# Gate and up of both FFNs by seven block products, with tokens in two phases

## The chip, the cores and the metric

The kernel runs on one core of a Trainium2 chip. The metric is device microseconds for one execution: the median of three runs before the change is 2480.66 us (2476.45 to 2481.32). Engines are TensorE (PE, with its weight loads as PEld), VectorE (DVE), ScalarE (ACT), GpSimd (POOL) and SyncE (SP), which issues most of the DMAs.

## The reference, cut to what matters

The reference is one layer of a decoder for 1024 prompt tokens and 64 sample tokens, that is 1088 rows x of 1024 channels, all float32:

```
x += 1/2 * SwiGLU_1(rms(x))
h = rms(x); [q | k | v | u | g_a | g_b] = h @ w_in
x += (sigmoid(g_a) * (A @ w_attn_branch) + sigmoid(g_b) * (B @ w_pool_branch)) @ w_out
x += 1/2 * SwiGLU_2(rms(x))

def _swiglu(x, w_up, w_down):
    gate, up = jnp.split(x @ w_up, 2, axis=-1)
    return (jax.nn.silu(gate) * up) @ w_down
```

A is a dilated attention and B a pooling over u; the change does not touch them. An FFN has 2816 hidden channels, so w_up is 1024 x 5632 and w_down 2816 x 1024. Key, value and pooling caches are copied to the outputs, in DMAs from DRAM to DRAM.

## The kernel before, in words

Channels lie on partitions and tokens on the free dimension. `xt` holds the residual as 8 blocks of 128 channels x 1088 tokens. Tokens are cut into three chunks, `CH`: 360, 360 and 368.

*Precision.* Each float32 operand is split into two float32r tiles: `hi` by an ACT copy, `lo` by a subtraction on DVE (`split`, lines 214 to 216; for the normed activations one in three is on POOL, line 341). `mm3` (lines 264 to 271) makes of each block pair three matmuls: hi x hi, hi x lo, lo x hi, summed in PSUM. So a block of 128 output channels with 1024 input channels costs 8 x 3 matmuls per chunk.

*Norm.* `norm` squares x on ACT, adds the squares on DVE and POOL, sums over partitions with small matmuls, takes the inverse root on DVE (`rsqrt`, 11 tiny operations) and writes a diagonal matrix `dg`; `normed` spreads it over partitions with one matmul and multiplies x, gain and that result on DVE, then splits it into `h_hi` and `h_lo`.

*FFN* (`ffn`, lines 344 to 432). Eleven steps `j`, each for 256 hidden channels: `wunit` loads gate's weights and splits them; six `gate` products (two halves x three chunks) go to PSUM tag `psa` and through Silu on ACT; `down` of the step before then adds its part to x (PSUM tag `psb`, one `scalar_tensor_tensor` on DVE for each of 8 blocks x 3 chunks); then `wunit` for up and six `up` products, which DVE multiplies with Silu's result and `split` stores as `hh`, `hl`. The last `down` goes chunk by chunk and calls `hook`, which starts the next norm or the outputs. PSUM tags `psa` and `psb` have four banks each.

*Memory.* `fp`, the FFN's pool, is opened on the right side after `bp` and `ip` are closed, the pools of the start (position biases: `tb`, `oh`, `fr`; input rows: `xn`, `sq`, `dg`), and so lies in their memory. `biases()` (line 444) makes four rows `fr` and POOL writes them to `f_scr`; 40 DMAs from there to `b_scr` are also on POOL's queue (lines 508 to 518).

*Order.* `Interleaver` puts steps of background jobs (norms, attention, fetches) between products, by costs in us that the code gives. A scheduler then orders the instructions of each engine: an instruction whose inputs are ready can be put ahead of earlier ones that wait; program order is its priority. Each engine and each DMA queue then runs in that order.

Output (`emit_outs`, line 1247): TensorE transposes x, DVE or ACT copies it, POOL and SP write it out.

Of the kernel before, what the change touches and what calls it, by code (L numbers as in the profile page):

```python
# [11 lines left out]
F32 = mybir.dt.float32  # L12
# [8 lines left out]
P = 128  # L21
# [8 lines left out]
CH = ((0, 360), (360, 360), (720, 368))  # L30
AW = 768
# [86 lines left out]
def body(ctx, tc, x_prompt, x_sample, c128, c512, c2048, state_pool, rel_bias_table,  # L118
# [182 lines left out]
    def norm(xt, c, gi):  # L301
        c0, n = CH[c]
# [24 lines left out]
        yield 5
        normed(xt, c, gi, dg)

    def normed(xt, c, gi, dg):  # L330

        c0, n = CH[c]
        r = psb()[:, :n]
        PE.matmul(r, ones, dg, start=True, stop=True)
# [9 lines left out]
    def ffn(xt, w_up, w_down, ncopy, hook):  # L344
        fctx = ExitStack()
        fp = fctx.enter_context(tc.tile_pool(name="fp", bufs=1, side="right"))

        def down(j, hh, hl, last):
            raws, pcs = [], {}
            for f in range(2):  # L350
                r = fp.tile([P, D], F32, tag="dr", name="dr", bufs=2)
                load(r, w_down[(2 * j + f) * P:(2 * j + f + 1) * P, :])
                raws.append(r)
            some_copies(ncopy)
            for dq in range(4):
                for f in range(2):
                    ph = fp.tile([P, 256], F32R, tag="dh", name="dh", bufs=8)
                    pl = fp.tile([P, 256], F32R, tag="dl", name="dl", bufs=8)
                    split(ph, pl, raws[f][:, dq * 256:(dq + 1) * 256])
                    pcs[dq, f] = (ph, pl)  # L360

            def one(d, c):
                c0, n = CH[c]
                o = psb()[:, :n]
                sl = slice((d % 2) * P, (d % 2 + 1) * P)
                mm3(o, [(pcs[d // 2, f][0][:, sl], pcs[d // 2, f][1][:, sl],
                         hh[:, f, c0:c0 + n], hl[:, f, c0:c0 + n]) for f in range(2)])
                xd = xt[:, d, c0:c0 + n]
                V.scalar_tensor_tensor(out=xd, in0=o, scalar=0.5, in1=xd, op0=ALU.mult, op1=ALU.add)  # L369
                il.advance(0.92)  # L370

            if last:
                for c in range(3):
                    for d in range(KD):
                        one(d, c)
                        hook(c, d)
            else:
                for d in range(KD):
                    for c in range(3):
                        one(d, c)  # L380

        def gate(w, f, c):
            o = proj(w, f, c, h_hi, h_lo)
            t = tmp()[:, :CH[c][1]]
            S.activation(t, o, AF.Silu)  # L385
            go()
            return t

        def up(w, f, c, t, hh, hl):
            c0, n = CH[c]  # L390
            o = proj(w, f, c, h_hi, h_lo)
            V.tensor_tensor(out=t, in0=t, in1=o, op=ALU.mult)  # L392
            split(hh[:, f, c0:c0 + n], hl[:, f, c0:c0 + n], t)
            go()

        def wblock(c0, pool):

            w = [pool.tile([P, KD, P], F32R, tag=x, name=x) for x in ("wh", "wl")]
            raw = wp.tile([P, KD, P], F32, tag="wr", name="wr", bufs=3)
            load(raw, w_up[:, c0:c0 + P].rearrange("(k p) n -> p k n", p=P))  # L400
            for k0 in range(0, KD, 4):
                split(w[0][:, k0:k0 + 4, :], w[1][:, k0:k0 + 4, :], raw[:, k0:k0 + 4, :])
            return w

        prev = None
        for j in range(11):
            sil = {}
            if prev is None:
                wg, wu = [wblock(0, wp)], [wblock(DFF, wp)]
            else:  # L410
                wg = wunit(w_up[:, j * 256:(j + 1) * 256])
                for f in range(2):
                    for c in range(3):
                        sil[f, c] = gate(wg, f, c)
                down(*prev, False)
                wu = wunit(w_up[:, DFF + j * 256:DFF + (j + 1) * 256])
            hh = fp.tile([P, 2, T], F32R, tag="hh", name="hh")
            hl = fp.tile([P, 2, T], F32R, tag="hl", name="hl")
            if prev is None:
                for c in range(3):  # L420
                    for f in range(2):
                        if len(wg) == f:
                            wg.append(wblock(P, wp))
                            wu.append(wblock(DFF + P, fp))
                        up(wu, f, c, gate(wg, f, c), hh, hl)
            else:
                for f in range(2):
                    for c in range(3):
                        up(wu, f, c, sil[f, c], hh, hl)
            prev = (j, hh, hl)  # L430
        down(*prev, True)
        fctx.close()

# [33 lines left out]
    for c, (c0, n) in enumerate(CH):  # L467
        tiles = range(3 * c, 3 * c + 3)
        for t in tiles:
            rows = P if t < 8 else NS  # L470
            sq = ip.tile([P, D], F32, tag="sq", name="sq", bufs=1)
            S.activation(sq[:rows], xns[t][:rows], AF.Square, accum_out=st[:rows, 0, t:t + 1])
# [13 lines left out]
        ts = slice(3 * c, 3 * c + 3)  # L486
# [3 lines left out]
        dg = ip.tile([P, 368], F32, tag="dg", name="dg", bufs=2)[:, :n]  # L490
        t0 = c0
        while t0 < c0 + n:
            t, a = t0 // P, t0 % P
            m = min(P - a, c0 + n - t0)
            V.tensor_scalar(out=dg[:, t0 - c0:t0 - c0 + m], in0=ident[:, a:a + m],
                            scalar1=st[:, 1, t:t + 1], scalar2=None, op0=ALU.mult)
            t0 += m
        normed(xt, c, 0, dg)
        if c == 2:
            biases()  # L500
# [26 lines left out]
    def hook1(c, d):  # L527
        if d < KD - 1:
            return
        spill(c)  # L530
        norms[c] = il.spawn(norm(xt, c, 1))
# [780 lines left out]
```

## Time and profile before

| | |
|---|---|
| median of 3 runs | 2480.66 us (2476.45 to 2481.32) |
| the profiled execution | 2476.46 us, span 2474.7 us, mean granted TensorE clock 0.98 |
| busy: PE, DVE, ACT, POOL | 2417.1, 1100.6, 616.6, 180.5 us |
| DMA | 259.11 MB, mean 105 GB/s |
| FFN1 | from the start to about 840 us |
| FFN2 | from about 1665 us to the end |

A row of a group of instructions names line, engine, operation, out<-in with the tile names (buffer numbers left out), shapes, count, then busy us and mean ns of one, then idle time before them. A row of a timeline gives start (us from the span's start), length in us, engine, line and count; in brackets the idle time before it and what ended it. Merged rows say x and a number; the length is then that of all. The record of an operation runs on for some 80 to 90 ns into the next on DVE, so operations back to back are closer than their length.

### The profile page before, as it was taken

To read this page: it belongs to the slowest core of one execution; us is meant where nothing else is said; L and a number is where in the kernel's file an instruction comes from. 1 tells how busy PE (TensorE), PEld (TensorE's weight loads), DVE (VectorE), ACT (ScalarE), POOL (GpSimd) and SP (SyncE) were. 2 spreads that over 40 slices of the span, in tenths; PEclk is the share of its full clock that TensorE was granted. 3 is DMA by queue.
4 is the path that set the end of the run, shared out by engine and by line. 5 is a ranking of instruction groups with operands and counts; after the bars stand their busy time and mean duration, and the time that the engine had idled before them with its cause. 6 is when DMAs were issued, how large, how long until landed. Compare 5 with 4: busy or idle time off the path is not lost.

```text
span 2474.7 us, 35899 instructions
## 1 busy us (share of the span) xinstructions
PE 2417.1 (98%) x14820; PEld 2364.7 (96%) x14820; DVE 1100.6 (44%) x2317; ACT 616.6 (25%) x1436; POOL 180.5 (7%) x304
## 2 busy tenths in 40 slices
PE   5999999999999899999899999999999999999999
PEld 4999999999999899999889799999999999999998
DVE  6244333333433743466677226545333333443334
ACT  5211111111111333434343132233111221111111
POOL 4200000000000211110011110011000000000001
PEclk7999999999999999999999999999999999999999
DMA  4411212222120223376654944710211222222132
GB/s 134 142 43 60 85 33 71 85 85 86 68 86 18 100 62 111 128 219 196 194 185 153 317 156 150 250 52 18 85 69 35 85 86 85 69 85 84 33 113 73
DMA packets 159571, 259.11 MB, mean 105 GB/s; under 512 B 14160, under 2 KB 128528, under 8 KB 158624
## 3 DMA queue, kind: packets, MB, share of 16 engines
q1 hardware_dynamic: 145392, 224.26, 27.8%
q0 software_dynamic: 14016, 32.56, 3.8%
q8 instruction: 116, 1.90, 0.3%
q14 instruction: 47, 0.39, 0.1%
HBM read 227.89 MB, written 76.32 MB: 123 GB/s over the span
## 4 chain that ended last, share of the span: by engine, by line
PE 85%; issue 6%; DVE 3%; DMA 3%; POOL 1%; ACT 1%; SPq 0%; POOLq 0%; DVEq 0%; ACTq 0%
PE psa L269 21%; PE psa L270 20%; PE psa L271 20%; PE psb L270 7%; PE psb L271 7%; PE psb L269 7%; DMA qb<-q_scr 1%; DMA u_scr<-us 1%; DMA wr<-in_ffn_w_up_dram 1%; DMA rt<-u_scr 1%; PE psb L745 1%; DVE qb L904 0%; PE psb L1065 0%; PE psb L879 0%; DVE sc L906 0%
## 5 line engine op out<-in xcount | busy, mean ns | idle before, releaser
L269 PE MATMUL psa<-h_hi,wh 128*128 128x360 f32 (+1 forms) x3216 | 1070.5, 333 | 22.9 <-DVE hl L216 13.1
L270 PE MATMUL psa<-h_lo,wh 128*128 128x360 f32 (+1 forms) x3216 | 1066.1, 332 | 5.3 <-DVE h_lo L341 5.1
L271 PE MATMUL psa<-h_hi,wl 128*128 128x360 f32 (+1 forms) x3216 | 1063.7, 331 | 0.0
L269 PEld LDWEIGHTS psa<-h_hi,wh 128*128 128x128 f32 x3216 | 612.0, 190 | 33.6 <-ACT wh L215 16.4
L270 PEld LDWEIGHTS psa<-h_lo,wh 128*128 128x128 f32 x3216 | 611.8, 190 | 10.9 <-DVE h_lo L341 5.9
L271 PEld LDWEIGHTS psa<-h_hi,wl 128*128 128x128 f32 x3216 | 611.4, 190 | 3.6 <-issue 2.8
L216 DVE TENSOR_TENSOR wl<-wr,wh 128x512 fp32r<-128x512 f32 (+1 forms) x284 | 185.9, 683 | 523.7 <-ACT wh L215 523.4
L369 DVE SCALAR_TENSOR_TENSOR xt<-psb,xt 128x360 f32<-128x360 f32 (+1 forms) x528 | 281.9, 534 | 262.5 <-PE psb L271 262.1
L269 PE MATMUL psb<-hh,dh 128*128 128x360 f32 (+1 forms) x1056 | 348.1, 330 | 0.0
L270 PE MATMUL psb<-hl,dh 128*128 128x360 f32 (+1 forms) x1056 | 348.1, 330 | 0.0
L271 PE MATMUL psb<-hh,dl 128*128 128x360 f32 (+1 forms) x1056 | 347.3, 329 | 0.0
L215 ACT ACTIVATE wh<-wr 128x512 fp32r<-128x512 f32 (+1 forms) x284 | 162.7, 618 | 381.4 <-PE psa L270 367.7
L269 PEld LDWEIGHTS psb<-hh,dh 128*128 128x128 f32 x1056 | 199.4, 189 | 0.3 <-DVE xt L369 0.2
L270 PEld LDWEIGHTS psb<-hl,dh 128*128 128x128 f32 x1056 | 198.9, 188 | 0.2
L271 PEld LDWEIGHTS psb<-hh,dl 128*128 128x128 f32 x1056 | 199.1, 189 | 0.0
L215 ACT ACTIVATE dh<-dr 128x256 fp32r<-128x256 f32 x176 | 72.3, 417 | 499.9 <-PE psb L270 486.5
L392 DVE TENSOR_TENSOR tmp<-tmp,psa 128x360 f32<-128x360 f32 x132 | 70.0, 531 | 224.2 <-PE psa L271 224.2
L215 ACT ACTIVATE hh<-tmp 128x360 fp32r<-128x360 f32 x132 | 66.0, 500 | 224.6 <-DVE tmp L392 214.7
L385 ACT ACTIVATE tmp<-psa 128x360 f32<-128x360 f32 x132 | 61.7, 467 | 239.8 <-PE psa L271 239.8
L216 DVE TENSOR_TENSOR hl<-tmp,hh 128x360 fp32r<-128x360 f32 x132 | 70.4, 534 | 46.2 <-ACT hh L215 46.1
L216 DVE TENSOR_TENSOR dl<-dr,dh 128x256 fp32r<-128x256 f32 x176 | 73.2, 421 | 26.0 <-ACT dh L215 23.3
L904 DVE TENSOR_TENSOR qb<-kt,qb 128x512 f32<-128x512 f32 x96 | 65.6, 685 | 34.0 <-DMA qb<-q_scr 34.0
(239 smaller groups left out, 1524.1 us busy)
## 6 DMA issues: line engine op xcount, KB each, us to landing
wr<-in_ffn_w_up_dram SPq DMA_DIRECT2D x88, 512.0 KB, 4.9
out_dram<-in_cache_kv_w_dram SPq DMA_DIRECT2D x32, 1020.0 KB, 9.3
qb<-q_scr SPq DMA_DIRECT2D x96, 256.0 KB, 4.3
dr<-in_ffn_w_down_dram SPq DMA_DIRECT2D x44, 512.0 KB, 4.1
wr<-in_w_in_dram SPq DMA_DIRECT2D x38, 512.0 KB, 4.8
kt<-in_cache_kv_w_dram SPq DMA_DIRECT2D x64, 256.0 KB, 4.1
vt<-in_cache_kv_w_dram SPq DMA_DIRECT2D x26, 512.0 KB, 6.4
t<-t_scr SPq DMA_DIRECT2D x16, 544.0 KB, 5.0
```

The source lines that it names most:

```text
L215: S.activation(hi, src, AF.Copy)
L216: V.tensor_tensor(out=lo, in0=src, in1=hi.bitcast(F32), op=ALU.subtract)
L269: PE.matmul(out, lh, rh, start=i == 0, stop=False)
L270: PE.matmul(out, lh, rl, start=False, stop=False)
L271: PE.matmul(out, ll, rh, start=False, stop=i == n - 1)
L369: V.scalar_tensor_tensor(out=xd, in0=o, scalar=0.5, in1=xd, op0=ALU.mult, op1=ALU.add)
L385: S.activation(t, o, AF.Silu)
L392: V.tensor_tensor(out=t, in0=t, in1=o, op=ALU.mult)
L745: PE.matmul(o[:rows, 4 * t + 2 * f:4 * t + 2 * f + 2], sqs[f][:, t * P:t * P + rows], halves, start=True, stop=True)
L904: V.tensor_tensor(out=qb, in0=kt.to_broadcast([P, 2, 256]) if g == 0 else kt, in1=qb, op=ALU.mult))
```

## The change

Gate and up of both FFNs are computed by Strassen's scheme. A unit is 256 hidden channels of gate or of up. Its weights are four blocks: channels in (two halves of 512, index 1 and 2 of the sum) by channels out (two of 128). The activations are four blocks: the same halves by two halves of a phase's tokens. Seven products of combinations replace eight. Tokens run in two phases: 512 (halves of 256) and 576 (halves of 288); all weights are loaded in each. `x` is normed for one phase at a time, and `right_sides` writes seven combinations x 4 blocks of 128 channels, split into hi and lo, in the memory of `h_hi` and `h_lo`. `prepare` forms four combinations of weights per unit on POOL, splits the left side of one product and keeps `LEAD` = 5 products ahead. The results are summed on DVE from PSUM. A pair is a gate unit and an up unit of the same channels; there are 11 pairs in a phase, 22 in an FFN. Down of the pair before is spread among the products, with its `lo` split on POOL and chunks of 512, or twice 288, tokens.

```
+PHASES = ((0, 256), (512, 288))
+LEAD = 5
+    def split(hi, lo, src, eng=V):
         S.activation(hi, src, AF.Copy)
+        eng.tensor_tensor(out=lo, in0=src, in1=hi.bitcast(F32), op=ALU.subtract)
...
+    def operand(p, q, k):
+        m = PHASES[p][1]
+        o = (4 * q + k) * m
+        return [x.rearrange("p k t -> p (k t)")[:, o:o + m] for x in (h_hi, h_lo)]
+    def right_sides(xt, gi, p, rs):
...
+        def parts(q, k, h, eng=V):
+            hi, lo = operand(p, q, k)
+            S.activation(hi, h, AF.Copy)
+            eng.tensor_tensor(out=lo, in0=h, in1=hi.bitcast(F32), op=ALU.subtract)
+        for k in range(4):
+            b11, b12, b21, b22 = half(k, 0), half(k, 1), half(k + 4, 0), half(k + 4, 1)
+            parts(0, k, b11)
+            t1 = less(b12, b11, V)
+            parts(1, k, b21)
+            t2 = less(b22, t1)
+            parts(3, k, t1)
+            t3 = less(b22, b12)
+            parts(2, k, t2)
+            t4 = less(b21, t2)
+            parts(4, k, t3)
+            parts(6, k, b22)
+            parts(5, k, t4, G)
+    def ffn(xt, gi, w_up, w_down, hook):
...
+        def prepare(i):
+            n, q = divmod(i, 7)
...
+            if q == 0:
+                s1s[n] = fp.tile([P, 4, P], F32, tag="s1", name="s1", bufs=1)
+                G.tensor_tensor(out=s1s[n], in0=a21, in1=a22, op=ALU.add)
+                G.tensor_tensor(out=a21, in0=a11, in1=a21, op=ALU.subtract)
+            src = (a11, a12, a11, s1s[n], a21, a22, a12)[q]
+            if q == 2:
+                G.tensor_tensor(out=a11, in0=s1s[n], in1=a11, op=ALU.subtract)
+                G.tensor_tensor(out=a12, in0=a12, in1=a11, op=ALU.subtract)
+            left[i] = [fp.tile([P, 4, P], F32R, tag=x, name=x, bufs=LEAD + 1) for x in ("sh", "sl")]
+            split(*left[i], src)
+            if q == 6:
+                del raws[n]
+                load_unit(n + 2)
...
+        def product(i, p):
+            while made[0] <= i + LEAD:
+                prepare(made[0])
+                made[0] += 1
+            lh, ll = left.pop(i)
+            bank = psa()[:, :PHASES[p][1]]
+            mm3(bank, [(lh[:, k, :], ll[:, k, :], *operand(p, i % 7, k)) for k in range(4)],
+                0.36)
...
+        for jj in range(22):
+            p, j = divmod(jj, 11)
+            t0, m = PHASES[p]
+            if j == 0:
+                if p:
+                    right_sides(xt, gi, p, [over_rows(diagonal(st, m)) for st in sts])
+                prev = None
...
+                a, b = tmp()[:, :m], tmp()[:, :m]
+                S.activation(a, product(7 * n, p), AF.Copy)
+                result(0, 0, product(7 * n + 1, p), a, True)
+                V.tensor_tensor(out=a, in0=a, in1=product(7 * n + 2, p), op=ALU.add)
+                V.tensor_tensor(out=b, in0=a, in1=product(7 * n + 3, p), op=ALU.add)
+                down_some(jj - 1, prev, (4 * kind, 4 * kind + 1))
+                o = product(7 * n + 4, p)
+                result(1, 1, o, b, True)
+                V.tensor_tensor(out=a, in0=a, in1=o, op=ALU.add)
+                if kind:
+                    down_weights(jj, 0)
+                down_some(jj - 1, prev, (4 * kind + 2, 4 * kind + 3))
+                if kind:
+                    down_weights(jj, 1)
+                result(1, 0, product(7 * n + 5, p), a, False)
+                result(0, 1, product(7 * n + 6, p), b, False)
+            prev = hid
+            if j == 10 and p == 0:
+                down_some(jj, prev, range(KD))
+            elif j == 10:
+                hook(jj, -1, 0)
...
```

`load_unit` loads a unit's weights in two DMAs of 512 KB into tag `ur` of `fp` (four buffers, two units). `result` adds the last term from PSUM on DVE and then, for gate, takes Silu on ACT; for up, it multiplies on DVE and splits with ACT and POOL. `down_weights` loads 512 KB and splits it in two steps of 512 with ACT and POOL. `sumsq` is the first half of `norm`; for phase 1 it runs during pair 1.

Around it: at the start the first four token tiles are normed, `right_sides` for FFN1's phase 0 comes, then the other five tiles are transposed, then `biases()` comes. Ahead of FFN2 the last step of `out_proj` starts `sumsq` for tokens 0 to 255 and 256 to 511 in place of the norms of three chunks, and `right_sides` follows. `hook1` starts the norms of the mixing layer once the last products are issued and after each of phase 1's two chunks of down; `emit_outs` writes tokens 0 to 511 out during phase 1 and uses `psb` and `tmp`.

## Rows read from the trace of the kernel before

**Rows 1.** The page: engine shares of part 1, DMA issues of part 6.
```profile
PE 2417.1 (98%) x14820; PEld 2364.7 (96%) x14820; DVE 1100.6 (44%) x2317; ACT 616.6 (25%) x1436; POOL 180.5 (7%) x304
...
wr<-in_ffn_w_up_dram SPq DMA_DIRECT2D x88, 512.0 KB, 4.9
```
**Rows 2.** Windows: start:end, length, busy us of each engine, clock, DMA.
```profile
200.00:600.00 400.00, 400.00 (x2423) 400.00 (x2422) 152.79 (x301) 73.76 (x156) 0.00 (x0) 1.00 0.21 73
1900.00:2400.00 500.00, 500.00 (x3027) 500.00 (x3026) 184.81 (x363) 92.12 (x194) 0.00 (x0) 1.00 0.23 79
61.70:66.40 4.70, 4.69 (x16) 4.70 (x17) 1.97 (x4) 1.60 (x5) 4.16 (x8) 0.50 1.00 339
840.00:880.00 40.00, 35.30 (x184) 33.93 (x185) 30.41 (x78) 15.74 (x34) 19.27 (x42) 0.87 0.16 54
1650.00:1710.00 60.00, 54.27 (x297) 52.55 (x296) 45.19 (x109) 22.76 (x47) 12.82 (x13) 0.91 0.06 18
```
**Rows 3.** The same for tile psa alone, up to 61.7 us.
```profile
0.00:61.70 61.70, 13.89 (x72) 12.55 (x72) 0.51 (x1) 0.94 (x2) 0.74 0.49 134
```
**Rows 4.** Timeline of TensorE in FFN1, first and last of two runs of matmuls.
```profile
300.04 0.33 PE L269 MATMUL psa<-h_hi,wh 128*128 128x368 f32 x1
...
301.54 0.33 PE L269 MATMUL psa<-h_hi,wh 128*128 128x368 f32 x1
...
302.55 0.32 PE L269 MATMUL psa<-h_hi,wh 128*128 128x360 f32 x1
...
303.86 0.33 PE L271 MATMUL psa<-h_hi,wl 128*128 128x360 f32 x1
```
**Rows 5.** Timeline of TensorE in the mixing layer, two-column matmuls.
```profile
971.42 1.81 PE L745 MATMUL psb<-halves,sqs 128*128 128x2 f32 x15
```
**Rows 6.** Groups by line and form, DVE and ACT.
```profile
L369 DVE SCALAR_TENSOR_TENSOR xt<-psb,xt 128x360 f32<-128x360 f32 x352 | 187.2, 532 | 208.8 <-PE psb L271 208.3
L216 DVE TENSOR_TENSOR wl<-wr,wh 128x512 fp32r<-128x512 f32 x276 | 182.8, 690 | 523.7 <-ACT wh L215 523.4
...
L216 DVE TENSOR_TENSOR dl<-dr,dh 128x256 fp32r<-128x256 f32 x176 | 73.2, 421 | 26.0 <-ACT dh L215 23.3 <-PE psb L270 0.3
...
L215 ACT ACTIVATE wh<-wr 128x512 fp32r<-128x512 f32 x276 | 160.2, 624 | 381.4 <-PE psa L270 367.7 <-DMA wr<-in_ffn_w_up_dram 10.1 <-DMA wr<-in_w_in_dram 2.4
```
**Rows 7.** Timelines of DVE and POOL, three places where both work.
```profile
838.33 1.09 DVE L310 TENSOR_TENSOR tmp<-tmp 128x360 f32<-128x360 f32 x1
839.34 0.52 DVE L341 TENSOR_TENSOR h_lo<-tmp,h_hi 128x360 fp32r<-128x360 f32 x1
...
838.08 0.95 POOL L341 TENSOR_TENSOR h_lo<-tmp,h_hi 128x360 fp32r<-128x360 f32 x1 [1.67 <-ACT h_hi L340]
...
873.62 2.35 DVE L341 TENSOR_TENSOR h_lo<-tmp,h_hi 128x368 fp32r<-128x368 f32 x5
...
873.57 3.23 POOL L341 TENSOR_TENSOR h_lo<-tmp,h_hi 128x368 fp32r<-128x368 f32 x1 [0.54 <-ACT h_hi L340]
...
1659.66 2.58 DVE L337 SCALAR_TENSOR_TENSOR tmp<-xt,gains,psb 128x360 f32<-128x360 f32 x5
...
1661.35 0.96 POOL L341 TENSOR_TENSOR h_lo<-tmp,h_hi 128x360 fp32r<-128x360 f32 x1 [4.11 <-PE psa L271]
```
**Rows 8.** Timelines of PE, ACT and POOL at the first FFN step.
```profile
61.71 0.67 PE L269 MATMUL psa<-h_hi,wh 128*128 128x360 f32 x1 [13.10 <-DVE hl L216]
...
60.63 0.50 ACT L215 ACTIVATE hh<-tmp 128x360 fp32r<-128x360 f32 x1 [9.87 <-DMA f_scr<-fr]
...
50.22 4.41 POOL L514 DMA_DIRECT2D b_scr<-f_scr  x8
...
58.22 1.09 POOL L455 DMA_DIRECT2D f_scr<-fr  x2
```
**Rows 9.** Timeline of DVE ahead of FFN2.
```profile
1642.60 1.30 DVE L216 TENSOR_TENSOR wl<-wr,wh 128x512 fp32r<-128x512 f32 x2 [1.79 <-ACT wh L215]
...
1663.57 0.53 DVE L1229 SCALAR_TENSOR_TENSOR xt<-psa,xt 128x368 f32<-128x368 f32 x1
```

More of the change, by code (lines that the diff above doesn't have):

```diff
@@ L382, in gate @@
[L382 to L430, printed above, removed]
@@ new lines, in ffn, with down_weights @@
+        made = [0]
+        def product(i, p):
[6 more added lines that the diff above has]
+                0.36)
+            il.advance(0.36)
+            return bank
+        def down_weights(jj, f):
+            r = wp.tile([P, D], F32, tag="wr", name="wr", bufs=3)
+            load(r, w_down[(2 * (jj % 11) + f) * P:(2 * (jj % 11) + f + 1) * P, :])
+            w = [wp.tile([P, D], F32R, tag=x, name=x) for x in ("wh", "wl")]
+            for a in range(2):
+                sl = slice(a * 512, (a + 1) * 512)
+                split(w[0][:, sl], w[1][:, sl], r[:, sl], G)
+            downs.setdefault(jj, []).append(w)
+            if f == 0:
+                some_copies(1)
@@ new lines, in down @@
+        def down(jj, hid, d, c0, n):
+            hh, hl = hid
+            t0 = PHASES[jj // 11][0]
+            o = psb()[:, :n]
+            sl = slice(d * P, (d + 1) * P)
+            mm3(o, [(downs[jj][f][0][:, sl], downs[jj][f][1][:, sl],
+                     hh[:, f, c0 - t0:c0 - t0 + n], hl[:, f, c0 - t0:c0 - t0 + n]) for f in range(2)])
+            xd = xt[:, d, c0:c0 + n]
+            V.scalar_tensor_tensor(out=xd, in0=o, scalar=0.5, in1=xd, op0=ALU.mult, op1=ALU.add)
+            il.advance(0.0026 * n)
@@ L466, in body @@
         xns.append(xn)
-    for c, (c0, n) in enumerate(CH):
-        tiles = range(3 * c, 3 * c + 3)
+    first = []
+    for tiles in ((0, 1), (2, 3), (4, 5, 6, 7, 8)):
         for t in tiles:
             rows = P if t < 8 else NS
-            sq = ip.tile([P, D], F32, tag="sq", name="sq", bufs=1)
-            S.activation(sq[:rows], xns[t][:rows], AF.Square, accum_out=st[:rows, 0, t:t + 1])
+            if t < 4:
+                sq = ip.tile([P, D], F32, tag="sq", name="sq", bufs=1)
+                S.activation(sq[:rows], xns[t][:rows], AF.Square, accum_out=st[:rows, 0, t:t + 1])
             for hf in range(2):
@@ L489, in body @@
         rsqrt(st[:, 0, ts], st[:, 1, ts], st[:, 2, ts])
[L490 to L500, printed above, removed]
+        dg = ip.tile([P, 256], F32, tag="dg", name="dg", bufs=2)
+        for i, t in enumerate(tiles):
+            V.tensor_scalar(out=dg[:, i * P:(i + 1) * P], in0=ident, scalar1=st[:, 1, t:t + 1],
+                            scalar2=None, op0=ALU.mult)
+        first.append(over_rows(dg))
+        if tiles[0] == 2:
+            right_sides(xt, 0, 0, first)
+    biases()
     ictx.close()
@@ L525, in spill, with hook1 @@
         G.dma_start(out=x_scr[:, :, c0:c0 + n], in_=xt[:, :, c0:c0 + n])
[L527 to L531, printed above, removed]
-    ffn(xt, ffn1_w_up[0], ffn1_w_down[0], 2, hook1)
+    def hook1(jj, i, d):
+        if i == -1:
+            spill(0)
+            norms[0] = il.spawn(norm(xt, 0, 1))
+        elif i is not None and d == KD - 1:
+            spill(i + 1)
+            norms[i + 1] = il.spawn(norm(xt, i + 1, 1))
+    ffn(xt, 0, ffn1_w_up[0], ffn1_w_down[0], hook1)
     qctx = ExitStack()
@@ L1275, in body, with hook2 @@
+    def hook2(jj, i, d):
+        if jj == 10 and d == KD - 1:
+            outs.extend((t, d) for d in range(0, KD, 2) for t in range(4))
+        elif i is None:
+            emit_outs(1)
+        elif i >= 0:
+            emit_outs(3)
+            if d % 2:
+                outs.extend((t, d - 1) for t in ((4, 5), (6, 7, 8))[i])
+    ffn(xt, 2, ffn2_w_up[0], ffn2_w_down[0], hook2)
+    emit_outs(len(outs))
     some_copies(len(copies))
```

183 lines of the change are left out of this document (108 added, 75 removed).

## The prediction

> **What bounds the kernel now.** I read the page's engine shares first, then the time in windows, then single matmuls. TensorE is busy in 98% of the span [rows 1], so only its columns and its stops count. In the middle of each FFN it takes 2423 matmuls in 400 us and 3027 in 500 us at the full clock (granted 1.00, the 2.4 GHz level) [rows 2]: 165.1 to 165.2 ns each, of 362.7 columns on average. DVE works 38% of such a window and POOL not at all. What is lost lies at three seams. At the start, 72 FFN matmuls (11.9 us of work) are done by 61.7 us, and the 4.7 us after that hold 16 matmuls at half clock instead of 28 [rows 2, 3]; the FFN thus begins as if at 61.7 - 11.9 + 2.0 = 51.8 us. Between FFN1 and the mixing layer 184 matmuls stand in 40 us, ahead of FFN2 297 in 60 us [rows 2], where 242 and 363 would fit: 9.6 and 10.9 us, less the time of a few small matmuls.
>
> **Price of one matmul.** Nine matmuls of 368 columns lie 1.50 us apart, eight of 360 columns 1.31 us [rows 4]: 166.7 and 163.8 ns. Eight columns cost 2.9 ns, about 8/2.4 = 3.3, and the rest is fixed: 165.2 - 362.7/2.4 = 14.1 ns. From this I estimate 256 columns at 120.8 ns, 288 at 134.1, 512 at 227.4. No row shows these widths for this type. From below the nearest row is a chain of 15 matmuls of two columns, each with fresh 128x128 weights: (1.81 - 0.25)/14 = 111.4 ns [rows 5]; so weights alone don't forbid 120.8. From above it is the 165.2 ns of today. I take the line through the two measured widths.
>
> The Trainium skill (TensorE: Matmul & The Clock Gate, section Back-to-back issue gap) gives N/2.4 + 2.5 ns for warm matmuls. That would be 152.5 ns at 360 columns; the trace has 163.8, so it disagrees by 11 ns. With 2.5 ns the narrower matmuls would save 116.8 us in place of the 104.6 below; it is a rival with a small chance.
>
> **The change, part by part.** *Products.* Gate and up of one FFN are 44 blocks x 8 x 3 chunks x 3 = 3168 matmuls now: x 165.2 = 523.4 us. After: 22 units x 7 products x 4 x 3 = 1848 per phase, at 120.8 and 134.1: 223.2 + 247.8 = 471.1 us. Saved 52.3 us per FFN, **104.6 us** in both. 17% more matmuls eat a part of the eighth that is saved in columns.
>
> *Down* keeps its columns: 1584 x 165.2 = 261.7 us before, 528 x 227.4 + 1056 x 134.1 = 261.7 after. No change.
>
> *Loads.* Both weights are read in each phase: 132 more transfers of 512 KB, 69 MB. An FFN window moves 73 to 79 GB/s [rows 2]; about 44 more are far below the 339 GB/s of the start. A load lands in 4.9 us [rows 1] and is issued a unit (8 us or more) ahead, so I cost it at nothing; without that cover it would be up to 5 us per unit.
>
> *Work of the other engines per pair* (one gate and one up unit). DVE: 14 weight splits x 690 ns = 9.7 us; 13 additions from PSUM and 4 products of 256 columns at about 420 each = 7.1; 8 additions of 512 into x at about 690 = 5.5; sum 22.4 us in phase 0, and in phase 1, with 288 columns at about 450 and 16 additions into x, 24.6 [rows 6]. ACT has less than that: 14 copies at 624 ns, and some 12 shorter ones [rows 6]. POOL gets 8 sums of weight blocks, 4 subtractions for down weights (512 elements) and 4 for the hidden values; 0.95 us per 360 elements [rows 7] makes 1.35 and 0.68: 18.9 us. TensorE has per pair 168 x 120.8 + 48 x 227.4 = 31.2 us in phase 0 and 168 x 134.1 + 96 x 134.1 = 35.4 in phase 1. Each engine by itself fits.
>
> But DVE and POOL shut each other out. A DVE subtraction of two SBUF tiles took 1.09 us where its like takes 0.52, because a POOL operation of 0.95 us had begun before it; and five such DVE operations in a row stretched one POOL operation to 3.23 us. Five DVE operations with an input from PSUM ran at their own pace (2.58 us, 0.50 apart) over a POOL one of 0.96 [rows 7]. So DVE's splits and products (11.4 us) and POOL's 18.9 exclude each other: 30.3 of 31.2 us in phase 0, 30.7 of 35.4 in phase 1. DVE's additions from PSUM (11 to 13 us) can lie beside POOL. Weights are split five products ahead (7 us) and four PSUM banks take up to three products of delay, so TensorE sees only what exceeds that. From below the cost is zero; from above all 18.9 us of POOL block DVE: 22.4 + 18.9 = 41.3, 10.1 us too much per pair. I take 0.8 us per pair for the 20 pairs of phase 0 that have down beside them (16 us), and 3 us for each of the 4 pairs that open a phase, where TensorE has 20 to 22 us of products alone against 30 (12 us): **28 us**.
>
> *Start.* `fp` now holds the raw weights, in the memory of `bp` and `ip`. Today its first tiles wait there: hh for 9.87 us on the DMAs from fr to f_scr, of which two are issued at 58.22, behind b_scr DMAs on POOL's queue (8 of them 4.41 us, 0.55 each); TensorE waits 13.1 us for it [rows 8]. After, the weights' load waits for the same DMA, and right_sides stands ahead of biases(): 44 DVE operations (some 19 us), of which 28 exclude 16 POOL ones (28 x 0.42 + 16 x 0.68 = 22.7 us). It can't begin before the norm of four token tiles, at 16 us or so. Then come 5 us of load, and POOL sums queue with 40 DMAs (22 us). From -6 to +25 us against the 51.8 of today; I take **+5**, nearer to today's 51.8 than to the late end, since fewer token tiles come first.
>
> *Turn of phases.* right_sides takes some 23 us; the last product needs the old operands, product 0 all four k of the new. Beside it lie products 2 to 6 and the down of pair 10 (10.9 us), if its first parts are issued early: the order does hoist, FFN2's first splits run at 1642.60, 21 us before the last addition of out_proj [rows 9]. 3 to 14 us each; I take 7, two of them: **14**. *Ahead of FFN2* the same 23 us stand behind out_proj in place of a chunk's norm, which costs 10.9 today; 0 to +20, taken **+6**. *Last down* of phase 1 waits for the last hidden values: addition, product, copy, subtraction (0.45 + 0.45 + 0.45 + 0.76 us), 2.5 with the releases, twice: **5**. The norms for the mixing layer and the tail keep their form: 0.
>
> **Sum.** The profiled execution took 2476.5 us (span 2474.7), 4.2 below the median of the runs. 2476.5 - 104.6 + 28 + 5 + 14 + 6 + 5 = **2430 us**. The seams' bounds alone give 2400 to 2465 for this case.
>
> **Rivals.**
> *Nothing waits*: POOL's operations fall beside DVE's reads of PSUM and into its idle 9 us per pair, and right_sides is issued early; seams cost 20: 2476.5 - 104.6 + 20 = 2392. For it: the spare time of both engines; against it: pairs that open a phase have no down beside them.
> *DVE and POOL become the bound* (slower): two thirds of POOL's 18.9 us block DVE, as the stretched rows suggest [rows 7]. Phase 0 takes 22.4 + 12.6 = 35.0 us per pair (+3.8), phase 1 24.6 + 12.8 = 37.4 (+2.0): 22 x 5.8 = 128 us. 2476.5 - 104.6 + 30 + 128 = 2530. It decides from 1.7 us of wait per pair on, averaged over 44 pairs (104.6 - 30 = 75). For it: both fill 97% of the pair in phase 0. Against it: DVE, at 72%, has 9 us to spare. The Trainium skill (SBUF — State Buffer, section Who interferes with whom) states it as a rule: two SBUF inputs on DVE against a GpSimd read are exclusive for the whole instruction, PSUM inputs not. The rows agree, 1.09 against 0.52 us.
> *Seams eat it* (right_sides is not hoisted, and POOL's DMAs stand ahead of its first sums): start +25, FFN2 +20, turns 14 each, 5 for the last downs, 28 between: 2476.5 - 104.6 + 106 = 2478, no change.
> *Narrow matmuls don't get cheaper* (165 ns at any width): 3696 x 165.2 in place of 3168, +87 us per FFN; 2476.5 + 174 + 30 = 2680. The slope of [rows 4] speaks against it.
> *The skill's fixed 2.5 ns*: 2418.
>
> **How the numbers follow.** Forecast 0.52; nothing waits 0.16; DVE and POOL 0.18; seams 0.11; dear narrow matmuls 0.02; the 2.5 ns 0.01. A measurement of this kernel can tell 0.2%, about 5 us. Faster: 0.51 + 0.16 + 0.01 + 0.02 of the seams = 0.70; within 0.2%: 0.01 + 0.05 of the seams = 0.06; slower: 0.18 + 0.04 + 0.02 = 0.24. The range 2385 to 2505 takes in the bounds of the waits up to half of the DVE and POOL case, and leaves out the rest of it, the dear matmuls and the lowest of the second: about 0.18.
>
> **What would show it.** Spacing of 121, 134 and 227 ns at 256, 288 and 512 columns. Products of about 224 and 248 us per phase, with the granted clock at 1.00. POOL operations longer than 1.35 us and DVE subtractions of 512 above 690 ns show the exclusion; if TensorE then waits for sl, s1 or a PSUM bank in every pair, the slower rival holds. Waits on f_scr ahead of the first ur load show the start. Gaps over 10 us at the turns, or spacings above 130 ns at 256 columns, would make the forecast wrong.

## The result and the profile after

The changed kernel takes 2517.72 us (median of 4 runs, 2516.5 to 2520.04), the kernel before 2478.55 in the same comparison: ratio 1.0161, 95% interval 1.0142 to 1.0181. The prediction was 2430 us, faster; it is slower by 39. The profiled execution took 2517.62 us, with a span of 2515.9.

The page of the changed kernel: engine shares and the weight loads.

```profile
PE 2363.3 (94%) x15894; PEld 2235.3 (89%) x15894; DVE 1817.6 (72%) x3246; ACT 975.9 (39%) x2130; POOL 1136.1 (45%) x1060
...
ur<-in_ffn_w_up_dram SPq DMA_DIRECT2D x176, 512.0 KB, 3.9
```

Against [rows 1], TensorE issues 1074 more matmuls and is yet busy for 54 us less; it is busy in 94% of the span, where it was 98%. So there is less work and more stopping. Windows of the changed kernel tell where (start:end, length, busy us and count of PE, PEld, DVE, ACT, POOL, then clock and DMA):

```profile
60.00:96.00 36.00, 0.61 (x3) 0.31 (x3) 1.06 (x3) 2.13 (x5) 19.56 (x28) 0.55 0.18 54
170.00:430.00 260.00, 260.00 (x1808) 241.94 (x1807) 220.06 (x337) 118.99 (x234) 174.83 (x133) 1.00 0.37 122
440.00:484.00 44.00, 29.67 (x94) 20.90 (x95) 32.63 (x51) 13.41 (x31) 23.02 (x25) 0.73 0.40 141
500.00:860.00 360.00, 359.06 (x2682) 356.73 (x2682) 301.28 (x488) 147.60 (x287) 202.01 (x159) 1.00 0.31 104
1702.00:1732.00 30.00, 19.62 (x54) 13.20 (x54) 27.40 (x64) 12.86 (x32) 14.97 (x17) 0.57 0.20 68
```

The two long windows are the middle of phase 0 and of phase 1, and answer to the first two of [rows 2]. In the first TensorE never stops, in the second for 0.94 us. 260/1808 = 143.8 ns per matmul makes 31.06 us for a pair of phase 0 (216 matmuls), 360/2682 = 134.2 makes 35.43 for one of phase 1 (264); forecast were 31.2 and 35.4. The other three are seams. From 60 to 96 us TensorE ran three matmuls, where a pair and more would have fitted.

**A ledger.** Down and products of an FFN take 11 x (31.06 + 35.43) = 731.4 us, where they took 4752 x 165.2 ns = 785.0 before: 53.6 us saved in each FFN, 107.2 in both. The rest of a stretch is lost time. A phase 0 should reach its last product 330.5 us after its start (10 pairs of 31.06, and 168 products of 118.5 ns), a phase 1 376.9 us (2808 x 134.2 ns) behind the 48 downs of 512 columns (11.1 us at 0.232 each). What the trace has beyond that, in us (before, FFN1's last down starts at 847.1 us, out_proj's last matmul at 1661.0 and FFN2's last down at 2465.7):

| | before | after | more | predicted more |
|---|---|---|---|---|
| FFN1, start | | 107.3 | | |
| FFN1, turn of phases | | 33.4 | | |
| FFN1, last downs | | 5.2 | | |
| FFN1 together | 62.1 | 145.9 | 83.8 | 28.5 |
| mixing layer (last down to last of out_proj) | 813.9 | 824.5 | 10.6 | 0 |
| FFN2, start | | 36.0 | | |
| FFN2, turn | | 36.2 | | |
| FFN2, last downs | | 4.5 | | |
| FFN2 together | 19.7 | 76.7 | 57.0 | 29.5 |
| tail behind the last down | 9.0 | 6.1 | -2.9 | 0 |
| work of both FFNs | | | -107.2 | -104.6 |
| span | 2474.7 | 2515.9 | 41.3 | -46.6 |

(Predicted for FFN1: 5 start, 7 turn, 2.5 last down, 14 exclusion; for FFN2: 6, 7, 2.5, 14. FFN2's turn holds some 3 us of transposes for the output as well.) The saving is all there. The seams lost 148.5 us more than before where 58 were foreseen.

**The start.** POOL of the changed kernel around the first products (start, length, line, count; in brackets the idle time before and what ended it):

```profile
48.99 1.13 POOL L639 DMA_DIRECT2D f_rep<-f_scr  x1
50.11 0.76 POOL L389 TENSOR_TENSOR tmp<-tmp 128x256 f32<-128x256 f32 x1
...
64.58 0.55 POOL L632 DMA_DIRECT2D b_scr<-f_scr  x1 [9.96 <-DMA f_rep<-f_scr]
...
77.20 1.25 POOL L639 DMA_DIRECT2D f_rep<-f_scr  x1
90.03 1.09 POOL L639 DMA_DIRECT2D f_rep<-f_scr  x1 [11.59 <-issue]
91.13 1.28 POOL L435 TENSOR_TENSOR s<-ur 128x512 f32<-128x512 f32 x1
```

and TensorE and ACT beside it:

```profile
54.62 0.58 PE L271 MATMUL psa<-h_hi,sh 128*128 128x256 f32 x1 [15.58 <-ACT sh L217]
...
95.12 0.63 ACT L217 ACTIVATE sh<-ur 128x512 fp32r<-128x512 f32 x1 [25.55 <-POOL ur L439]
95.80 0.58 PE L271 MATMUL psa<-h_hi,sh 128*128 128x256 f32 x1 [35.39 <-ACT sh L217]
```

The first product starts at 54.62 us, and products 0 and 1, which need no sum of weights, run. Product 2 needs POOL's sums, and the first of those (L435) stands on POOL's queue behind all 44 DMAs that copy f_scr: three to f_rep and 41 to b_scr, which the description of the kernel and the expectations count as 40. Of the three to f_rep the first takes 15.3 us to land, and a later DMA on the queue waits 9.96 us for that (64.58); behind the second, which takes 12.3 us, POOL idles for 11.59 us before the third (90.03). What stands behind a waiting DMA waits with it. The split of product 2 then waits for POOL's sums (95.12), and TensorE in all 35.39 us. Those waits are no news: POOL of the kernel before has them too, later, and there nobody needed POOL.

```profile
79.49 1.10 POOL L521 DMA_DIRECT2D f_rep<-f_scr  x1 [0.69 <-issue]
92.09 1.10 POOL L521 DMA_DIRECT2D f_rep<-f_scr  x1 [11.50 <-issue]
```

**The turn of phases**, TensorE of the changed kernel and then DVE:

```profile
442.63 1.66 PE L271 MATMUL psb<-hh,wh 128*128 128x512 f32 x4 [4.58 <-ACT hh L217]
445.91 0.79 PE L272 MATMUL psb<-hl,wh 128*128 128x512 f32 x1 [1.62 <-POOL hl L218]
458.13 1.13 PE L351 MATMUL psb<-tmp,ones 128*128 128x288 f32 x4
459.98 0.40 PE L271 MATMUL psa<-h_hi,sh 128*128 128x288 f32 x1 [0.71 <-ACT h_hi L394]
```
```profile
433.12 1.17 DVE L335 TENSOR_SCALAR tmp<-ident,nst 128x128 f32<-128x128 f32 x6
...
458.94 1.35 DVE L382 SCALAR_TENSOR_TENSOR tmp<-xt,gains,psb 128x288 f32<-128x288 f32 x3
```

The diagonals of the new phase's norm are ready at 434 us, but the matmuls that spread them (L351) run at 458.13, behind all 48 downs of pair 10. Only then does right_sides begin. So the downs and right_sides stand one behind the other, and the window from 440 to 484 us holds 94 matmuls at a mean granted clock of 0.73.

**Ahead of FFN2** the same in small. out_proj's last matmul starts at 1701.69 us; TensorE of the changed kernel then:

```profile
1705.67 0.85 PE L351 MATMUL psb<-tmp,ones 128*128 128x256 f32 x2 [3.65 <-DVE tmp L335]
...
1710.10 1.22 PE L351 MATMUL psb<-tmp,ones 128*128 128x256 f32 x2 [2.95 <-DVE tmp L335]
```

The matmuls that spread the two norms wait 3.65 and 2.95 us for DVE's diagonals, and the first product comes at 1710.94.

### The profile page after: what moved, and what is told of

Read it like the earlier page. It is cut to its first block, busy times and chain, and to the rows that moved or that the text cites. A ratio compares the mean times of both kernels' runs of the same rounds, so it can differ in the third digit from the quotient of the medians.

```text
span 2515.9 us, 42145 instructions
## 1 busy us (share of the span) xinstructions
PE 2363.3 (94%) x15894; PEld 2235.3 (89%) x15894; DVE 1817.6 (72%) x3246; ACT 975.9 (39%) x2130; POOL 1136.1 (45%) x1060
## 5 line engine op out<-in xcount | busy, mean ns | idle before, releaser
L271 PE MATMUL psa<-h_hi,sh 128*128 128x256 f32 (+1 forms) x2464 | 724.9, 295 | 62.1 <-ACT sh L217 51.0
L272 PE MATMUL psa<-h_lo,sh 128*128 128x256 f32 (+1 forms) x2464 | 727.9, 295 | 18.7 <-DVE h_lo L395 18.3
L273 PE MATMUL psa<-h_hi,sl 128*128 128x256 f32 (+1 forms) x2464 | 723.1, 294 | 0.0
L218 DVE TENSOR_TENSOR sl<-ur,sh 128x512 fp32r<-128x512 f32 x528 | 589.5, 1123 | 109.9 <-ACT sh L217 99.9
L271 PEld LDWEIGHTS psa<-h_hi,sh 128*128 128x128 f32 x2464 | 474.2, 193 | 77.4 <-ACT sh L217 52.8
L272 PEld LDWEIGHTS psa<-h_lo,sh 128*128 128x128 f32 x2464 | 474.7, 193 | 33.6 <-DVE h_lo L395 29.3
L273 PEld LDWEIGHTS psa<-h_hi,sl 128*128 128x128 f32 x2464 | 475.6, 193 | 0.5 <-DVE sl L218 0.5
L272 PE MATMUL psa<-h_lo,wh 128*128 128x360 f32 (+1 forms) x1104 | 374.7, 339 | 5.5 <-DVE h_lo L364 5.5
L271 PE MATMUL psa<-h_hi,wh 128*128 128x360 f32 (+1 forms) x1104 | 376.6, 342 | 3.4 <-ACT h_hi L363 3.4
L273 PE MATMUL psa<-h_hi,wl 128*128 128x360 f32 (+1 forms) x1104 | 370.9, 336 | 0.0
L271 PEld LDWEIGHTS psa<-h_hi,wh 128*128 128x128 f32 x1104 | 213.6, 194 | 10.6 <-issue 5.0
L272 PEld LDWEIGHTS psb<-hl,wh 128*128 128x128 f32 x1056 | 200.7, 190 | 22.4 <-POOL hl L218 8.6
```

The lines of the kernel that those rows point to most:

```text
L218: eng.tensor_tensor(out=lo, in0=src, in1=hi.bitcast(F32), op=ALU.subtract)
L271: PE.matmul(out, lh, rh, start=i == 0, stop=False)
L272: PE.matmul(out, lh, rl, start=False, stop=False)
L273: PE.matmul(out, ll, rh, start=False, stop=i == n - 1)
```

## The experiments

Two theories stood against each other. **S**: the time is lost at the seams, by the order of instructions on POOL's queue (start), TensorE's queue (turns) and DVE's (FFN2); in the pairs nothing waits. **X**, which the prediction had held for its slower side: DVE and POOL shut each other out all along. Each experiment is the changed kernel with the edit that is shown.

**1. right_sides of phase 1 ahead of the last down of phase 0.**

```
-                if p:
-                    right_sides(xt, gi, p, [over_rows(diagonal(st, m)) for st in sts])
...
             if j == 10 and p == 0:
+                right_sides(xt, gi, 1, [over_rows(diagonal(st, PHASES[1][1])) for st in sts])
                 down_some(jj, prev, range(KD))
```

> right_sides of phase 1 is issued ahead of the down of pair 10 instead of behind it. Theory S (the loss lies at the seams, and is a matter of what stands ahead of what in a queue): TensorE's matmuls that spread the norm no longer wait behind 48 down matmuls, so DVE's 25 us of right_sides runs beside 11 us of down; each turn loses 22 to 24 us instead of 33, the time is about 2497 us. Theory X (the loss is the exclusion of DVE and POOL, wherever both are loaded; order matters little): the same DVE and POOL operations take as long, the time stays within 5 us of 2518.

Measured: 2492.68 us (2489.56 to 2494.26), ratio to before 1.0059 (1.0041 to 1.0078). In the ledger the turns fall from 33.4 and 36.2 us to 23.0 and 24.4, by 10.4 and 11.8: the 11 us of the downs now lie beside right_sides. TensorE of this kernel:

```profile
438.01 1.13 PE L351 MATMUL psb<-tmp,ones 128*128 128x288 f32 x4
441.02 0.40 PE L271 MATMUL psa<-h_hi,sh 128*128 128x288 f32 x1 [1.88 <-ACT h_hi L394]
```

That is within S's 22 to 24 us but for 0.4; X falls for this seam. What stays, 23 us each, goes with right_sides: from 437.90 to 461.00 DVE is busy without a stop.

**2. The three f_rep DMAs to SyncE, in the pairs.** They are put in a list and issued in `hook1`.

```
-    for g in (0, 1, 3):
-        G.dma_start(out=f_rep[g], in_=fbias(g, 0, [[BL, 4], [0, P], [1, BL]]))
+    late = [(f_rep[g], fbias(g, 0, [[BL, 4], [0, P], [1, BL]])) for g in (0, 1, 3)]
...
     def hook1(jj, i, d):
+        if i is None and jj >= 1:
+            for _ in range(min(3, len(late))):
+                o, a = late.pop(0)
+                nc.sync.dma_start(out=o, in_=a)
```

> The three f_rep DMAs go to SP's queue, and only after the first pair; the b_scr DMAs stay on POOL. S: POOL's first weight sums come 20 to 25 us earlier, at about 67 us in place of 91, since two waits of 10 and 12 us on POOL's queue go; 2495 us. X: POOL's sums and the splits still exclude each other, 2513 to 2518 us.

Measured: 2501.36 us (2496.54 to 2504.66), 1.0094 (1.0073 to 1.0115); the start loses 88.8 us in place of 107.3. S holds, short by 6 us. The 41 b_scr DMAs are still ahead of POOL's sums.

**3. The 41 b_scr DMAs as well**, in the same list.

> The 40 b_scr DMAs that read f_scr go to SP's queue too, after the first pair. S: POOL's first sums follow the first landing of raw weights at about 53 us, the second product no longer waits 36 us; 35 us less than the changed kernel, 2483 us. X: 2513 to 2518 us.

Measured: 2493.26 us (2493.11 to 2496.33), 1.0066 (1.0048 to 1.0084); start 81.8. Better, but 10 us short. SyncE's queue says why for 5.8 of the 10:

```profile
35.99 0.74 SPq L649 DMA_DIRECT2D f_rep<-f_scr  x1
36.79 6.60 SPq L649 DMA_DIRECT2D b_scr<-f_scr  x6
44.46 0.61 SPq L649 DMA_DIRECT2D f_rep<-f_scr  x1
48.42 5.39 SPq L649 DMA_DIRECT2D b_scr<-f_scr  x6
54.01 5.53 SPq L191 DMA_DIRECT2D ur<-in_ffn_w_up_dram  x4
```

Though written in the pairs, these DMAs were ready early and were put ahead of the first weight loads, which went out at 54.01 us in place of 48.22. The queue had changed, the fault not.

**4. The norm ahead of FFN2 one chunk earlier.** The squares of tokens 0 to 255 and 256 to 511 are summed behind chunks 0 and 1 of out_proj in place of 1 and 2.

```
-                if c:
+                if c < 2:
                     st = stat()
-                    pend[c] = (st, il.spawn(sumsq(xt, (c - 1) * 256, 256, st)))
+                    pend[c + 1] = (st, il.spawn(sumsq(xt, c * 256, 256, st)))
```

> Ahead of FFN2 the sums of squares of tokens 0 to 255 and 256 to 511 start after chunks 0 and 1 of the last out_proj step in place of chunks 1 and 2. S: right_sides no longer waits 8 us for the second norm and starts with the end of out_proj: about 8 us less, 2510 us. X: within 3 us of 2518.

Measured: 2514.75 us (2508.6 to 2518.74), 1.015 (1.0122 to 1.0178); the interval overlaps that of the changed kernel, so the time alone decides nothing. The ledger has 33.4 us for FFN2's start in place of 36.0, 2.6 less. TensorE of this kernel, where out_proj ends at 1699.73:

```profile
1703.71 1.22 PE L351 MATMUL psb<-tmp,ones 128*128 128x256 f32 x2 [3.22 <-DVE tmp L335]
1706.43 0.58 PE L271 MATMUL psa<-h_hi,sh 128*128 128x256 f32 x1 [1.28 <-ACT h_hi L394]
```

So the norm was late, but right_sides behind it costs the more. By itself the edit gives less than the 8 us of S; with the others it gives more: kernel 10, which has it, loses 30.5 us here and kernel 9, which has not, 37.8. Why isn't shown.

**5. The late DMAs behind the weight loads.** As in 3, with an order that holds each DMA behind the last load issued.

```
+                with tc.issue_after(last_load[0].ins):
+                    nc.sync.dma_start(out=o, in_=a)
```

> The three f_rep and 40 b_scr DMAs go to SyncE in the pairs, as before, but each now stands behind the last weight load issued so far, so they can't go ahead of the ur loads. Theory S (the start is lost because POOL's weight sums stand behind DMAs on POOL's queue): the ur loads are issued at about 48 us again, the sums begin at about 55, the time lost up to 170 us falls from 97 to about 58, and the kernel takes about 2480 us (2472 to 2488). Rival M (the start is set by when fp's memory comes free and by POOL's own work, its queue matters no more): not better than the last version with these DMAs on SyncE, about 2493.

Measured: 2485.49 us (2480.12 to 2494.85), 1.0034 (1.0018 to 1.005). Inside S's range (2472 to 2488), 5 us over its 2480, with times that spread over 15 us. POOL's sums begin at 54.76 us, as S has it. The interval just touches that of experiment 3, so by the time alone M is unlikely but not out. TensorE now has a new stop of 17 us at 160 us. SyncE, then an ACT row within the stop and the TensorE row that ends it:

```profile
127.30 13.72 SPq L650 DMA_DIRECT2D f_rep<-f_scr  x3
141.06 18.40 SPq L650 DMA_DIRECT2D b_scr<-f_scr  x9
159.57 0.38 SPq L191 DMA_DIRECT2D wr<-in_ffn_w_down_dram  x1
```
```profile
166.83 0.63 ACT L217 ACTIVATE sh<-ur 128x512 fp32r<-128x512 f32 x1 [12.85 <-DMA ur<-in_ffn_w_up_dram]
177.54 0.79 PE L272 MATMUL psb<-hl,wh 128*128 128x512 f32 x1 [16.79 <-POOL hl L218]
```

Twelve DMAs in a row occupied SyncE for 32 us, and the loads of wr and ur stood behind them; ACT's split waited 12.85 us for the ur load. The cost had moved a second time.

**6. A lead of two products.** `LEAD = 2` in place of 5.

> The changed kernel with LEAD = 2 in place of 5: only two products' left sides are ready ahead of TensorE. If the lead of five is what hides the 20 exclusions of DVE and POOL of phase 0 and the 1.5-us sums, TensorE now waits in the pairs: a pair of phase 0 grows from 31.1 us to 32 to 33, and the kernel takes 2535 to 2560 us. Rival: the exclusion is hidden without the lead (DVE and POOL have slack within each product): pairs stay at 31.1 and 35.4 us, and the kernel is within 5 us of 2518.

Measured: 2533.72 us (2530.51 to 2535.11), 1.0221 (1.0206 to 1.0237), 16 us slower than with five, where 2535 was the foot of the range. Its windows:

```profile
170.00:430.00 260.00, 259.26 (x1774) 236.98 (x1773) 225.96 (x327) 116.20 (x230) 175.45 (x130) 1.00 0.37 118
500.00:860.00 360.00, 359.94 (x2665) 355.71 (x2665) 297.39 (x486) 147.17 (x287) 205.05 (x158) 1.00 0.32 106
```

A pair takes 31.66 and 35.66 us, 0.60 and 0.23 more than with a lead of five: 22 x 0.83 = 18 us over both FFNs; 32 to 33 us had been expected for phase 0, so the effect is there but smaller. TensorE's short waits in the first window end with splits of weights (sl) and of hidden values (hh). So work does come late to a product, and the lead of five hides it. The rival, slack enough without the lead, falls. The run does not tell the exclusion of DVE and POOL from their mere load.

**7. All mended seams together**, 1, 4 and 5, and one block of the last spread down held back behind the last product:

```
+                last = j == 10 and kind
-                down_some(jj - 1, prev, (4 * kind + 2, 4 * kind + 3))
+                down_some(jj - 1, prev, (6,) if last else (4 * kind + 2, 4 * kind + 3))
...
+                if last:
+                    down_some(jj - 1, prev, (7,))
```

> All mended seams together: right_sides of phase 1 issued ahead of the last down of phase 0, the late DMAs on SyncE behind the weight loads, the second norm's squares one chunk earlier, and one block of the last spread down held back behind the last product. Theory S adds the parts up: 2518 - 25 (turns) - 38 (start) - 3 (ahead of FFN2) - 4 (last down) = 2448 us (2435 to 2465), faster than the kernel before. Rival: TensorE's stops are not independent, a gain at one seam comes back at the next, and it is over 2465.

Measured: 2468.22 us (2465.34 to 2470.83), 0.9957 (0.994 to 0.9974). Faster than before, but 20 us over the sum and 3 over its range, on the rival's side. 16 of the 20 are the stop of experiment 5, which is here too (16.09 us at 158 us) and which the sum, written before that run, had left out; a gain that comes back at the next seam, as the rival has it, the ledger does not show. The block held back gave nothing: the last downs take 7.0 and 6.4 us from the last product on, 1.6 of it the held block itself, where 5.2 and 4.5 stood.

**8. The same with biases() ahead of the first right_sides.**

```
         if tiles[0] == 2:
+            biases()
             right_sides(xt, 0, 0, first)
-    biases()
```

> The same with biases() ahead of the first right_sides, so that f_scr's DMAs, which hold back fp's memory and with it the first ur loads, are done earlier. Theory S: first product at about 47 to 50 us in place of 54.6, kernel about 2442 us (6 less than without). Rival: the position biases then delay right_sides on ACT and DVE by as much as they give: within 3 us of the version without, or slower.

Measured: 2465.34 us (2461.85 to 2468.51), 0.9947 (0.9932 to 0.9962). The first product starts at 50.88 us against 50.59 without. By 3 us and with overlapping intervals, it can't be told from no gain; the rival fits better.

**9. The start alone, with the late DMAs spread.** As in 5, one DMA for every second block of the spread down, the three of f_rep apart.

```
+    late = small[:4] + late[:1] + small[4:8] + late[1:2] + small[8:12] + late[2:] + small[12:]
...
+        if i is None and jj >= 1 and d % 2 == 0:
+            for _ in range(min(1, len(late))):
```

> The changed kernel with one edit: the 43 late DMAs (f_rep, b_scr) on SyncE, each behind the last weight load, one for every second block of the spread down, and the three of f_rep apart from each other. The version that sent three at a time lost 17 us more at 160 us, where a load of ur stood behind 32 us of such DMAs. Theory S: without that stop the kernel takes 2468 us (2462 to 2476), faster than before, so the DMAs ahead of POOL's sums alone are some 50 of the 2518. Rival: the DMAs cost their time wherever they stand on a queue that carries loads, and it stays at 2480 or more.

Measured: 2469.41 us (2463.84 to 2471.26), 0.9963 (0.995 to 0.9975). POOL of this kernel, and the window in which the changed kernel had three matmuls:

```profile
51.70 1.28 POOL L435 TENSOR_TENSOR s<-ur 128x512 f32<-128x512 f32 x1 [5.19 <-DMA ur<-in_ffn_w_up_dram]
```
```profile
60.00:96.00 36.00, 31.81 (x216) 29.80 (x215) 35.65 (x54) 20.84 (x48) 24.20 (x20) 0.87 0.30 89
```

The sums start at 51.70 us in place of 91.13, the window holds 216 matmuls, and the start loses 65.4 us in place of 107.3. By the medians this edit is worth 48 of the 2518 us, inside S's range, and by the ledger 42 of them lie at the start. So these DMAs alone made the change slower than no change.

**10. All seams, with the DMAs spread.** 1, 4, 7, 8 and 9.

> All mended seams with biases() first and the late DMAs spread in this way: 2465 less the 15 us of the stop at 160 us, 2450 us (2443 to 2457). Rival: as for the start alone, within 4 us of 2465.

Measured: 2448.14 us (2445.1 to 2451.36), 0.988 (0.9862 to 0.9898). It beats both kernels, the one before by 1.2%.

**11. One more split of right_sides on POOL**, on top of 10.

```
-            parts(4, k, t3)
+            parts(4, k, t3, G)
```

> The same with one more of the seven lo splits in right_sides (that of t3) on POOL in place of DVE: 4 of 44 DVE operations of a seam move. Theory D: the 22 us of right_sides at each of the four seams are DVE's own time (44 operations of some 0.41 us and the first splits of weights), so a seam gets up to 1.6 us shorter and the kernel 3 to 7 us faster than without. Theory X, what the prediction held: DVE and POOL exclude each other, so the moved work comes back on DVE: no gain, or up to 10 us slower.

Measured: 2447.72 us (2447.03 to 2450.41), 0.9878 (0.9857 to 0.9898): no gain, as X says. The 22 us behind the first product of FFN2 in kernel 10, then in kernel 11:

```profile
1649.00:1671.00 22.00, 17.59 (x50) 12.32 (x51) 22.00 (x45) 12.33 (x31) 12.53 (x15) 0.50 0.04 17
```
```profile
1655.00:1677.00 22.00, 17.10 (x54) 13.24 (x55) 22.00 (x42) 13.33 (x32) 16.28 (x19) 0.50 0.06 19
```

DVE is busy for all 22 us in both, once with 45 operations and once with 42; POOL's time grows from 12.53 to 16.28. The four seams of the ledger lose 144.4 us in kernel 10 and 143.3 in 11, where D would have up to 6.4 less. DVE's subtractions of two SBUF tiles in this seam show where the work went, kernel 10 and then 11:

```profile
L389 DVE TENSOR_TENSOR tmp<-tmp 128x256 f32<-128x256 f32 x4 | 1.7, 414 | 0.0
```
```profile
L389 DVE TENSOR_TENSOR tmp<-tmp 128x256 f32<-128x256 f32 x4 | 3.3, 815 | 0.0
```

DVE had less to do, and what it had took longer. TensorE gets some 50 matmuls into 22 us, at half clock.

## Why the prediction was wrong

The ledger of the experiments, in us beyond the work as above:

| | start | turn 1 | FFN2 start | turn 2 | time |
|---|---|---|---|---|---|
| changed kernel | 107.3 | 33.4 | 36.0 | 36.2 | 2517.72 |
| 1, right_sides first | 107.4 | 23.0 | 36.6 | 24.4 | 2492.68 |
| 4, norm earlier | 105.3 | 33.1 | 33.4 | 35.5 | 2514.75 |
| 9, DMAs spread | 65.4 | 33.2 | 37.8 | 36.6 | 2469.41 |
| 10, all | 65.9 | 22.4 | 30.5 | 25.6 | 2448.14 |

**Price of one matmul: right.** Spacing of the changed kernel, first and last of three runs of matmuls:

```profile
299.73 0.28 PE L272 MATMUL psa<-h_lo,sh 128*128 128x256 f32 x1
...
302.93 0.28 PE L272 MATMUL psa<-h_lo,sh 128*128 128x256 f32 x1
...
303.52 0.40 PE L271 MATMUL psb<-hh,wh 128*128 128x512 f32 x1
...
304.46 0.39 PE L272 MATMUL psb<-hl,wh 128*128 128x512 f32 x1
```
```profile
699.72 0.30 PE L272 MATMUL psa<-h_lo,sh 128*128 128x288 f32 x1
...
702.12 0.30 PE L272 MATMUL psa<-h_lo,sh 128*128 128x288 f32 x1
```

27 matmuls in 3.20 us are 118.5 ns, 18 in 2.40 are 133.3, and 4 of 512 columns in 0.94 are 235 (0.232 is the median of 352). Forecast from [rows 4]: 120.8, 134.1, 227.4. Saved were 107.2 us, against 104.6. The rival of dear narrow matmuls falls. So does the rival with the Trainium skill's fixed 2.5 ns (TensorE: Matmul & The Clock Gate, section Back-to-back issue gap): by it 256 columns would take 109.2 ns. The section gives the formula for an isolated matmul, which the prediction left out.

**Loads: right in the pairs.** The windows of the pairs move 122 and 104 GB/s, and a load lands in 3.9 us. The price named for lost cover, up to 5 us, was too low where it was lost: experiment 5 lost 17 us once, when a load stood behind 32 us of other DMAs.

**DVE and POOL: right in kind, the 28 us wrong in the pairs.** Groups of the changed kernel from 170 to 860 us (count, then busy us and mean ns):

```profile
L218 DVE TENSOR_TENSOR sl<-ur,sh 128x512 fp32r<-128x512 f32 x231 | 261.7, 1139 | 30.6 <-ACT sh L217 25.7
...
L218 POOL TENSOR_TENSOR wl<-wr,wh 128x512 fp32r<-128x512 f32 x78 | 114.9, 1493 | 17.3 <-ACT wh L217 17.3
```

A split that takes 690 ns with POOL idle [rows 6] takes 1139 on average with POOL at work, and POOL's 1493 where 1350 was the estimate. The 1.09 us of [rows 7] belong to an addition (L310, 0.53 at the median), not to a subtraction; that changes nothing. That the two slow each other agrees with the Trainium skill (SBUF — State Buffer, section Who interferes with whom), which calls the two exclusive. But TensorE felt none of the 16 us put on the 20 pairs of phase 0: it ran without a stop, and the prediction's lower bound, zero, was the value. Experiment 6 shows what hides the late work: the lead of five. The 12 us put on the pairs that open a phase lie inside the seams, and no run separates them. The exclusion does bite where nothing is ahead, in right_sides at the seams (experiment 11). Rival X as a rule for the whole kernel, which gave 2530, fell, though the time came near to it.

**Start: the step that failed most.** It set +5, at most +25, over the 51.8 us of before; by the ledger it is 107.3 - 51.8 = +55. The prediction did write that POOL's sums queue with 40 DMAs, and weighed it as part of a range. It left out the three f_rep DMAs on the same queue, two of which held it for 9.96 and 11.59 us, and its reason for staying near 51.8, fewer token tiles, bears on the first product alone: that came at 54.62, but product 2, the first that needs POOL, at 95.80. With the DMAs out of the way (9) the start is 65.4, or +14: inside the range. Its other term was right: the first ur load goes out at 48.22, after the last DMA from fr to f_scr has landed at 48.16.

**Turns: failed.** 7 us each were set, 14 the upper bound, and 3 for the pair that opens the phase; 33 and 36 came. The prediction let products 2 to 6 of the old phase and the down of pair 10 lie beside right_sides. The down could, but wasn't: 10 to 12 us (1). The products weren't either: right_sides stands behind the last product in the program and overwrites operands that this product reads. Even in experiment 1 the matmuls that spread its norm start at 438.01, behind the last product's last matmul at 437.89, so 23.0 and 24.4 us stay open. The evidence named for early issue, splits that ran 21 us early [rows 9], was of work with memory of its own. Splitting right_sides, so that the parts for product 0 come while product 6 still runs, wasn't tried.

**Ahead of FFN2: mis-sized.** FFN2's start and end take 40.5 us against 19.7 of before, 20.8 more, where 6 + 2.5 were set and +20 was the start's upper bound. The order of the norm is 2.6 of it alone (4) and 7.3 between kernels 9 and 10; right_sides at half clock is the rest by its window, not by a run of its own.

**Last downs: near.** 5.2 and 4.5 us behind the last product, 2.5 each forecast beside an unstated remainder of before. **Mixing layer: 0 forecast, +10.6.** The trace has TensorE waiting 5.46 us for the norm's h_lo there, where a chunk's norm lay under downs before; this wasn't tried, and between the kernels of the experiments the stretch varies by 10 us (818.6 to 828.0).

Of the rivals, "seams eat it" had the mechanism, both halves of it: right_sides not hoisted, and POOL's DMAs ahead of its first sums. It gave them 25 and 14 us, where 55 and 33 to 36 were right, and a chance of 0.11. The sum's own bounds were too narrow as well: taken together, -6 to +25 at the start, 3 to 14 at each turn and 0 to 20 ahead of FFN2 give 2405 to 2478, not 2400 to 2465.

## What to carry to other kernels

When an engine that was idle gets work that the bottleneck waits for, list everything that is on its queue already, with the wait of each entry, since harmless waits become the bound; moving such entries to another queue helps in full only if they are held behind the loads there, and spread (2493, 2485 and 2469 us here). Price a seam by the work that has no other work to lie beside: what overwrites an operand can't begin before its last reader, whatever the order. An exclusion between two engines cost nothing here where operands were made five products ahead; where nothing was ahead, moving work from one of the two to the other gained nothing.

## What the runs showed of the hardware

A DMA of f_rep (896 KB from DRAM to DRAM, issued on POOL) took 12.3 to 15.3 us to land in the changed kernel. POOL's next instruction was not held: a subtraction ran at once behind the first (50.11), and the first sum behind the third (91.13). Held were later DMAs on the same queue, for 9.96 and 11.59 us, and what stood behind them. On SyncE in experiment 9 one f_rep took 0.64 us of the queue and the DMA behind it 4.08; three of f_rep and nine of b_scr in a row held that queue for 32 us (5).

In the three seams shown of the changed kernel the granted clock fell, to means of 0.55, 0.73 and 0.57. Ahead of FFN2 in kernels 10 and 11 it was 0.50, the lower of the two levels (1.2 GHz), for the 22 us of right_sides, where TensorE had been busy without a stop before out_proj's end (43.00 of the 43 us up to 1643 in kernel 10). So its matmuls, though few, ran at half speed, which shows in lengths of 0.41 to 0.58 us against 0.28 for 256 columns.
